# High and low weight parts interleaved in one buffer, at a walking place

## The chip, the cores and the metric

The program runs on one core of one Trainium2 chip. The metric is the device time in microseconds (us) of one execution; smaller is better.

## The reference

One row of 256 tokens of width 2048 passes through two blocks. The first mixes four branches (a gated linear attention, a gated linear recurrence, a compressed and sliding attention, a delta-rule recurrence), gates and sums them, and adds a convolved, gated feed-forward layer of width 5632. The second has two layers, each with two kinds of attention. All numbers are float32. Nearly all the arithmetic is products of the normalized activations with large weight matrices:

```
w_in     2048 x 16016      (all branches' inputs, and the four gates of 2048)
w_branch 4 x 512 x 2048    w_out 2048 x 2048
ffn_up   2048 x 11264      ffn_down 5632 x 2048
w_in_2   2 x 2048 x 2048   w_out_2 2 x 512 x 2048
y = rms_norm(x, g) @ w_in;  ...;  x = x + merged @ w_out;  x = x + ffn(x);  ...
```

## The kernel before

Activations lie transposed: features on the 128 partitions, tokens along the free dimension. To keep float32 accuracy at the rate of the shorter format `F32R`, each operand is split into a high part (the value rounded to `F32R`) and a low part (what is left), and a product is formed as high x high + high x low + low x high. For activations both parts lie in one tile: `act` is [128, 16, 2, 256], with part 0 high and part 1 low; `ys`, `ff_s` and `l_ys` are built alike.

Weights come from HBM in pieces of 128 partitions x 1024 floats (512 KB), packed beforehand in the order of use, by the generator `wchunk`. For each piece it issues a DMA on SP's queue into `raw` (four buffers), lets ScalarE write the high part `hi` (tile name `whi`, line 311 by way of `cp_s`), and lets VectorE write the low part `lo` = raw - hi (tile name `wlo`, line 299 by way of `tt`). `hi` and `lo` are separate tiles, three buffers each, 1088 floats per partition; a piece uses 1024 of them, from a starting place that `where` chooses. A buffer is written again once its last reader is done. The scheduler places these instructions by a priority that `rank` sets, so that the splitting runs ahead of the products.

`gemmT` uses the pieces as stationary operands, 128 weight columns at a time, with the activations as the moving operand. In the wide form (`w_gate`, `ffn_up`, `ffn_down`, `w_out`) one product moves both parts of the activations, 512 columns, past the high weights, and one moves the high part, 256 columns, past the low weights: a pair. In the narrow form (mixer inputs, branch outputs, second block) there are three products of 256 columns: a triple. Every product loads its weights anew. A piece of 1024 columns holds eight such pairs or triples. All products go through `mm`, line 293, into PSUM tiles `o`. `half_out` and the end of `proj_out` take pieces and form triples in the same way.

`gemm_tok` is the other way round: the activations are stationary and the pieces move, 512 columns at a time (272 in the case of one matrix), each activation block three times. It calls `wchunk` without a form.

`where` gives the starting places of `hi` and `lo` in floats. A table `AT` holds, for each activation tile, the place of that tile modulo 256 bytes; the places of the parts are at fixed distances from it, 64 and 192 bytes in the narrow form, 192 and 0 in the wide one. Without a form both are 0.

In between, as Python generators advanced by `tick` after each k, stand the small products and elementwise chains of the branches (`rwkv`, `lru`, `gla2`, `nsa2`, the attentions). One of them is of use below: in `gla2`, `factors` forms differences and products over halves of blocks of length L; at its last level, L = 1, its operands are every second float.

Of the kernel before, what the change touches and what calls it, by code (L numbers as in the profile page):

```python
# [9 lines left out]
F32R = mybir.dt.float32r  # L10
# [245 lines left out]
class Net:  # L256
# [100 lines left out]
    def wchunk(self, src, nk, n, form=None):  # L357

        kp = max(1, 1024 // n)
        if len(self.boot) > 4:  # L360
            kp = 2
        for k0 in range(0, nk, kp):
            kn = min(kp, nk - k0)
            for _ in range(kn // 2 if self.boot else 0):
                self.boot.pop(0)()
            with self.rank(20 * self.place):
                raw = self.raw.tile([128, 1024], F32, tag="raw", name="raw")[:, :kn * n]
                self.nc.sync.dma_start(raw, src[:, k0 * n:(k0 + kn) * n])
                a, b = self.where(form)
                hi = self.ws.tile([128, 1088], F32R, tag="hi", name="whi")[:, a:a + kn * n]  # L370
                lo = self.ws.tile([128, 1088], F32R, tag="lo", name="wlo")[:, b:b + kn * n]
                self.cp_s(hi, raw)
                self.tt(lo, raw, hi.bitcast(F32), OP.subtract)
            if self.place >= 0:
                self.place = self.place + 1 if self.place < 20 else -1
            yield k0, hi.rearrange("p (k n) -> p k n", n=n), lo.rearrange("p (k n) -> p k n", n=n)


    AT = {"act": 128, "ff_s": 224, "ys": 224, "l_ys": 160}

    def where(self, form):

        if form is None:
            return 0, 0
        name, wide = form
        return tuple((self.AT[name] + d) % 256 // 4 for d in ((192, 0) if wide else (64, 192)))

    def gemmT(self, src, act=None, wide=False, name="act"):

# [1355 lines left out]
```

## Time and profile before

| | |
|---|---|
| median of 2 runs | 1925.53 us (1925.04 to 1926.01) |
| the profiled execution's own time | 1919.65 us |
| its span, first to last instruction | 1917.8 us |
| busy: TensorE / its weight loads / VectorE / ScalarE / GpSimd | 98% / 89% / 73% / 54% / 4% |
| granted TensorE clock | 0.995 |
| read from HBM | 343.52 MB, 181 GB/s over the span |

The profiled execution is one run of the program under the hardware profiler. Busy shares are shares of the span. Matmuls overlap one another in the records, so the rate of TensorE is read from the distance between starts and not from durations.

### The profile page before, as it was taken

Reading aid. Unit: us, or ns where it says so; the run is one execution under the profiler, and the core shown is the slowest. Engines: PE = TensorE matmul, PEld = TensorE weight load, DVE = VectorE, ACT = ScalarE, POOL = GpSimd, SP = SyncE. Lnnn points to the kernel's source line nnn. Section 1 sums busy time; section 2 is a strip of 40 time slices with the busy share of each in tenths; the row PEclk is TensorE's granted clock in tenths of the full one; section 3 lists DMA queues with packets and bytes.
Section 4 is the critical chain, followed back from the end, with each engine's and each line's share of the span. In section 5 each row is a group of like instructions: output and inputs, shape, how many; then the busy total and the mean of one; then the engine's idle time right before and its main releaser. Section 6 shows DMA issues by size and latency. Waiting matters only on the chain.

```text
span 1917.8 us, 31880 instructions
## 1 busy us (share of the span) xinstructions
PE 1878.6 (98%) x12558; PEld 1701.4 (89%) x12558; DVE 1407.4 (73%) x2211; ACT 1034.8 (54%) x1542; POOL 80.9 (4%) x107
## 2 busy tenths in 40 slices
PE   8999999999999999999999999999999999999997
PEld 8999889999789999988888888888888888999886
DVE  8888967687776666675888787556888876768766
ACT  6565444465555444454655555334555554546574
POOL 0000010000000000002000000000000011003002
PEclk9999999999999999999999999999999999999999
DMA  7545553355644555565556555555555555654533
GB/s 273 188 154 181 193 143 111 121 167 169 225 144 150 191 196 190 196 230 192 194 193 193 197 191 193 195 193 188 197 195 194 192 196 193 210 165 152 192 124 108
DMA packets 98262, 348.48 MB, mean 182 GB/s; under 512 B 11200, under 2 KB 12224, under 8 KB 97984
## 3 DMA queue, kind: packets, MB, share of 16 engines
q1 hardware_dynamic: 93888, 336.15, 52.7%
q10 hardware_dynamic: 3600, 8.73, 1.3%
q0 software_dynamic: 624, 1.57, 0.4%
q8 instruction: 98, 1.61, 0.4%
q14 instruction: 52, 0.43, 0.1%
HBM read 343.52 MB, written 2.88 MB: 181 GB/s over the span
## 4 chain that ended last, share of the span: by engine, by line
PE 90%; DVE 5%; ACT 3%; DMA 1%; issue 1%; SPq 0%; POOL 0%; DVEq 0%; ACTq 0%
PE o L293 83%; DVE wlo L299 2%; ACT whi L311 1%; ACT L308 1%; DMA nsa_w<-in_cmp 1%; PE rw_u L293 0%; PE lg L1313 0%; PE rw_y L293 0%; PE rw_p L293 0%; PE gla_s L293 0%; DVE x L299 0%; PE l_o L293 0%; PE pt L318 0%; PE nsa_o L293 0%; PE rw_n L293 0%
## 5 line engine op out<-in xcount | busy, mean ns | idle before, releaser
L293 PE MATMUL o<-act,whi 128*128 128x512 f32 (+1 forms) x4736 | 1293.9, 344 | 6.0 <-ACT whi L311 6.0
L299 DVE TENSOR_TENSOR wlo<-raw,whi 128x1024 fp32r<-128x1024 f32 (+2 forms) x634 | 770.3, 1216 | 366.3 <-ACT whi L311 356.9
L293 PE MATMUL o<-act,wlo 128*128 128x256 f32 x3712 | 1034.3, 279 | 4.6 <-DVE wlo L299 4.5
L311 ACT CAST whi<-raw 128x1024 fp32r<-128x1024 f32 (+2 forms) x634 | 659.5, 1041 | 645.0 <-PE o L293 522.1
L293 PEld LDWEIGHTS o<-act,whi 128*128 128x128 f32 x4736 | 819.1, 189 | 113.8 <-ACT whi L311 6.5
L293 PEld LDWEIGHTS o<-act,wlo 128*128 128x128 f32 x3712 | 699.3, 188 | 9.5 <-DVE wlo L299 7.5
L293 PE MATMUL o<-ff_s,whi 128*128 128x512 f32 x704 | 239.5, 389 | 0.0
L293 PE MATMUL o<-ff_s,wlo 128*128 128x256 f32 x704 | 194.3, 276 | 0.0
L293 PEld LDWEIGHTS o<-ff_s,whi 128*128 128x128 f32 x704 | 132.2, 188 | 27.1
L293 PEld LDWEIGHTS o<-ff_s,wlo 128*128 128x128 f32 x704 | 132.2, 188 | 0.0
L299 POOL TENSOR_TENSOR acc<-acc,sq 128x256 f32<-128x256 f32 x56 | 58.7, 1049 | 1230.8 <-ACT sq L308 1228.6
L311 ACT COPY evh<-o 128x256 f32<-128x256 f32 x152 | 56.4, 371 | 97.9 <-PE o L293 97.8
L293 PE MATMUL o<-ys,whi 128*128 128x256 f32 x512 | 92.3, 280 | 0.0
L299 DVE TENSOR_TENSOR evh<-o,evh 128x256 f32<-128x256 f32 x152 | 64.0, 421 | 34.9 <-ACT evh L311 34.8
L293 PEld LDWEIGHTS o<-ys,whi 128*128 128x128 f32 x512 | 78.1, 188 | 1.9 <-issue 0.6
L293 PE MATMUL o<-whi,act 128*128 128x512 f32 (+1 forms) x256 | 74.0, 371 | 0.0
L305 DVE SCALAR_TENSOR_TENSOR ff_u<-hup,vec,ff_u 128x256 f32<-128x256 f32 x176 | 73.4, 479 | 0.0
L293 PE MATMUL o<-ys,wlo 128*128 128x256 f32 x256 | 71.7, 280 | 0.0
L308 ACT ACT_TABLE_LOAD x48 | 61.6, 1283 | 2.0 <-PEq L1733 1.2
L299 DVE TENSOR_TENSOR x<-o,x 128x256 f32<-128x256 f32 (+1 forms) x113 | 45.5, 454 | 14.5 <-PE o L293 8.9
L293 PEld LDWEIGHTS o<-whi,act 128*128 128x128 f32 x256 | 46.4, 188 | 8.8 <-issue 0.5
L308 ACT ACTIVATE ff_u<-hup,vec 128x256 f32<-128x256 f32 x88 | 48.0, 592 | 2.0 <-DVE hup L299 2.0
(427 smaller groups left out, 1407.9 us busy)
## 6 DMA issues: line engine op xcount, KB each, us to landing
raw<-in_ffn_up SPq DMA_DIRECT2D x176, 512.0 KB, 3.6
raw<-in_w_gate SPq DMA_DIRECT2D x128, 512.0 KB, 3.9
raw<-in_w_mix SPq DMA_DIRECT2D x78, 512.0 KB, 3.7
raw<-in_ffn_down SPq DMA_DIRECT2D x48, 512.0 KB, 3.4
raw<-in_w SPq DMA_DIRECT2D x48, 512.0 KB, 3.7
raw<-in_w_br SPq DMA_DIRECT2D x32, 512.0 KB, 4.3
raw<-in_w_out SPq DMA_DIRECT2D x32, 512.0 KB, 4.4
raw<-in_ffn_down2a SPq DMA_DIRECT2D x32, 512.0 KB, 3.5
```

The costliest lines, as they stand in the source:

```text
L293: self.nc.tensor.matmul(out, lhsT, rhs, start=start, stop=stop, skip_group_check=True)
L299: (eng or self.nc.vector).tensor_tensor(out, a, b, op=op)
L305: self.nc.vector.scalar_tensor_tensor(out, a, s, b, op0=op0, op1=op1)
L308: self.nc.scalar.activation(out, a, f, **k)
L311: self.nc.scalar.copy(out, a)
```

## The change

`hi` and `lo` become two views of one tile of [128, 1056, 2]: float 2i of a partition is the high part of weight i, float 2i + 1 its low part. Both are so read and written by steps of 8 bytes. The tile has three buffers, as each of the two had. `where` now returns one place, in pairs of 8 bytes: the activation tile's own place plus 40 bytes for each piece that has asked before, modulo 256 bytes; so 32 consecutive pieces of `gemmT`, `half_out` and `proj_out` start at 32 different places. Pieces without a form stay at 0.

```diff
-                a, b = self.where(form)
-                hi = self.ws.tile([128, 1088], F32R, tag="hi", name="whi")[:, a:a + kn * n]
-                lo = self.ws.tile([128, 1088], F32R, tag="lo", name="wlo")[:, b:b + kn * n]
+                a = self.where(form)
+                both = self.ws.tile([128, 1056, 2], F32R, tag="hl", name="whl")[:, a:a + kn * n]
+                hi, lo = both[:, :, 0], both[:, :, 1]
                 self.cp_s(hi, raw)
                 self.tt(lo, raw, hi.bitcast(F32), OP.subtract)
...
+    count = 0
     AT = {"act": 128, "ff_s": 224, "ys": 224, "l_ys": 160}
 
     def where(self, form):
 
         if form is None:
-            return 0, 0
-        name, wide = form
-        return tuple((self.AT[name] + d) % 256 // 4 for d in ((192, 0) if wide else (64, 192)))
+            return 0
+        self.count += 1
+        return (self.AT[form[0]] + 8 * (5 * self.count % 32)) % 256 // 8
```

## Rows read from the trace of the kernel before

**Rows 1.** The page's first part: busy us (share of the span) xinstructions.
```profile
PE 1878.6 (98%) x12558; PEld 1701.4 (89%) x12558; DVE 1407.4 (73%) x2211; ACT 1034.8 (54%) x1542; POOL 80.9 (4%) x107
```
**Rows 2.** The page's fourth part, the chain that ended last, by line.
```profile
PE o L293 83%; DVE wlo L299 2%; ACT whi L311 1%; ACT L308 1%; DMA nsa_w<-in_cmp 1%; PE rw_u L293 0%; PE lg L1313 0%; PE rw_y L293 0%; PE rw_p L293 0%; PE gla_s L293 0%; DVE x L299 0%; PE l_o L293 0%; PE pt L318 0%; PE nsa_o L293 0%; PE rw_n L293 0%
```
**Rows 3.** TensorE's groups by line and form: xcount | busy us, mean ns | idle before.
```profile
L293 PE MATMUL o<-act,wlo 128*128 128x256 f32 x3712 | 1034.3, 279 | 4.6 <-DVE wlo L299 4.5
L293 PE MATMUL o<-act,whi 128*128 128x512 f32 x2688 | 928.3, 392 | 0.0
...
L293 PE MATMUL o<-ff_s,whi 128*128 128x512 f32 x704 | 239.5, 389 | 0.0
L293 PE MATMUL o<-ff_s,wlo 128*128 128x256 f32 x704 | 194.3, 276 | 0.0
...
L293 PE MATMUL o<-ys,wlo 128*128 128x256 f32 x256 | 71.7, 280 | 0.0
L293 PE MATMUL o<-whi,act 128*128 128x512 f32 x192 | 60.6, 394 | 0.0
...
L293 PE MATMUL o<-wlo,act 128*128 128x512 f32 x96 | 37.9, 394 | 0.0
L293 PE MATMUL o<-l_ys,wlo 128*128 128x256 f32 x128 | 35.5, 277 | 0.0
```
**Rows 4.** Timeline of TensorE, wide form, starts 24 pairs apart: start us, us, what.
```profile
899.82 0.39 PE L293 MATMUL o<-act,whi 128*128 128x512 f32 x1
...
907.98 0.39 PE L293 MATMUL o<-act,whi 128*128 128x512 f32 x1
```
**Rows 5.** The core's span and mean granted TensorE clock.
```profile
core 0: 1917.8 us, clock 0.995
```
**Rows 6.** Timeline of TensorE: three triples, four, then `act` pairs: three, four.
```profile
545.65 0.40 PE L293 MATMUL o<-ys,whi 128*128 128x256 f32 x2
...
546.72 0.39 PE L293 MATMUL o<-ys,whi 128*128 128x256 f32 x2
...
548.08 0.39 PE L293 MATMUL o<-ys,whi 128*128 128x256 f32 x2
...
548.42 0.40 PE L293 MATMUL o<-act,whi 128*128 128x512 f32 x1
...
549.48 0.39 PE L293 MATMUL o<-act,whi 128*128 128x512 f32 x1
...
550.84 0.39 PE L293 MATMUL o<-act,whi 128*128 128x512 f32 x1
```
**Rows 7.** Timeline of TensorE, wide form, starts eight pairs apart.
```profile
556.55 0.40 PE L293 MATMUL o<-act,whi 128*128 128x512 f32 x1
...
559.35 0.40 PE L293 MATMUL o<-act,whi 128*128 128x512 f32 x1
```
**Rows 8.** The tile `whi`, 900 to 1600 us: ns min/median/max; idle us, times, until.
```profile
L299 DVE TENSOR_TENSOR wlo<-raw,whi x258: 1209/1226/1229, 899.7 to 1599.7; 128x1024 fp32r<-128x1024 f32 x129
L311 ACT CAST whi<-raw x257: 1032/1050/1056, 901.3 to 1598.6; 128x1024 fp32r<-128x1024 f32 x129
its engine sat idle before it (us, times) until:
  PE o L293: 195.0, 131
```
**Rows 9.** The tile `gla_E`, all levels L together: ns min/median/max.
```profile
L299 DVE TENSOR_TENSOR gla_E<-gla_b x16: 412/418/425, 414.0 to 439.7; 128x256 f32<-128x256 f32 x16
```
**Rows 10.** Who waited for whom on TensorE: us in total, times, longest us.
```profile
PE o L293 <- ACT whi L311: 6.0, 2, 5.3
PE o L293 <- DVE wlo L299: 4.7, 7, 0.9
```
**Rows 11.** Timeline of TensorE in `gemm_tok`, starts 12 products apart.
```profile
1812.83 0.62 PE L293 MATMUL o<-whi,act 128*128 128x512 f32 x2
...
1815.61 0.39 PE L293 MATMUL o<-whi,act 128*128 128x512 f32 x1
```

## The prediction

> **What bounds the kernel now.** I began with the page's busy times: TensorE is busy 98% of the span, VectorE 73%, ScalarE 54% [rows 1]. Since a busy TensorE need not be one at its peak, I went on to the chain that ended last: 83% of the span is TensorE in line 293 on the output tiles `o`, which are the weight products [rows 2]. The groups by line and form give their number and sort [rows 3]: 2688 + 704 = 3392 wide pairs (a high product of 512 columns and a low one of 256) and, from the remaining low products, 3712 + 704 + 256 + 128 - 3392 = 1408 narrow triples (high, high, low, 256 columns each). Both come to 768 columns, so I speak of 4800 groups. Besides them 288 products of `gemm_tok` have the weights as the moving operand, 512 columns each; 96 more, by the code (16 k, two token halves, three products), have 272.
>
> The time of a group is read in the timeline from start to start, since durations overlap. In the long even stretch 24 wide pairs take 907.98 - 899.82 = 8.16 us, 340 ns each [rows 4]. [...] Yet a triple at its best also takes 340 ns: four in 548.08 - 546.72 = 1.36 us [rows 6]. So 340 ns is what the moving stream of 768 four-byte columns costs when nothing disturbs it. 4800 x 0.340 = 1632 us: most of the kernel already stands at this floor.
>
> But the same instructions also run slower, and this is what matters here. Behind a pause eight wide pairs take 559.35 - 556.55 = 2.80 us, 350 ns each [rows 7]. In one `ys` gemm the first three triples take 546.72 - 545.65 = 1.07 us (357 ns each), the next four 340; the wide pairs behind it take 353 for three, then 340 [rows 6]. Instructions, sizes and places are the same; only the moment at which weight load and moving stream meet differs. The products find their even step after a few groups, or they don't. I read it as a dependence on how the two reads of SBUF stand to each other; the code's fixed places modulo 256 bytes hold that relation constant from piece to piece.
>
> **The change, part by part.** No instruction, byte of HBM or DMA is added or removed. What changes is the step of four accesses from 4 to 8 bytes (ScalarE's write of the high part, VectorE's read of it and its write of the low part, TensorE's read of both), the place of a piece relative to the moving operand (40 bytes further each piece, all 32 places in 32 pieces), and that the two parts come free together.
>
> *Splitting.* The cast takes 1.05 us and the subtraction 1.23 us per piece [rows 8], while a piece feeds TensorE for 8 x 0.34 = 2.72 us. VectorE's steps of 8 bytes are shown: the GLA factor products include one level (L = 1) that reads and writes every second float, and all 16 calls lie between 412 and 425 ns [rows 9]. So 0 for VectorE. ScalarE has no such row; between nothing and a doubled cast (2.1 us, still inside 2.72; 1035 + 634 x 1.05 = 1700 us in all, under the span) I take nothing, as VectorE's row is the nearest. The cover is the lead of three buffers: over the whole run TensorE waits 6.0 us for high parts and 4.7 us for low ones [rows 10], and of 257 casts in the middle of the run 131 had to wait until TensorE freed a buffer [rows 8], so they run as far ahead as the buffers let them. Taking both parts as one buffer means that a high product may wait until the low part is written, about 1.2 us later; with such a lead that is hidden nearly everywhere. If it isn't in the lean pieces, I put it at up to 12 us, twice the wait for high parts. Taken: 0.
>
> *Weight load by steps of 8 bytes.* A load of 128 weights now covers 1024 bytes of a partition instead of 512. No load in this trace is strided. The nearest row is the moving stream: it sustains 256 x 4 = 1024 bytes in 113 ns (340/3). If the load's port does the same, the load still fits behind a 256-column product, just; if it fetches half as fast (227 ns), it is exposed behind every 256-column product. That would be 113 ns in a pair and 3 x 113 = 340 in a triple: 383 + 479 = 862 us. These are the ends; I am near the low one, because the moving stream's row is the same memory and engine at the same rate. [...]
>
> *The walking place.* What held the even step was a fixed relation; now each piece (8 groups) brings another. Bounds: all pieces fall in step at once, 0; none does, 4800 x 10 ns (350 against 340) = 48 us, or 58 us at 352; three groups lost per piece and then the even step, about 40 ns x 602 pieces = 24 us. The load also meets the moving stream on twice as many bytes, so up to twice that, some 115 us. Weight load and walking place are two readings of one contention, not to be added in full: I take **52 us** for both.
>
> [...]
>
> *Weights as the moving operand.* In `gemm_tok` 12 products take 1815.61 - 1812.83 = 2.78 us, 232 ns each [rows 11]; these pieces were unplaced before and still are. Read by steps of 8 bytes they sweep 4096 bytes, twice the rate that any row shows. Ends: nothing, and doubled, 288 x 0.232 = 67 us plus 96 x 272/512 x 0.232 = 12 us, 79 us in all. No row is near; I take the low end for the sum and keep the other as a rival.
>
> **Sum.** 0 + 0 + 52 + 0 = 52 us. On the profiled execution's own time of 1919.65 us (span 1917.8 and 1.85 around it): 1971.7. The median shown, 1925.53, is 5.9 above that execution: 1977.6, say **1978 us**, 2.7% slower. About 2% (38 us) is what a measurement here tells from no change.
>
> **The rivals.**
> (1) Not slower. The loads keep pace and each piece falls in step within a group or two: 0 to 30 us, 1923 to 1955. For it: steps of 8 bytes cost VectorE nothing, the even step was reached from several starts [rows 6]. Against it: eight pairs in a row without finding the step [rows 7]. [...] It decides at 8 ns a group (38 us over 4800): below that, no difference.
> (2) Dearer, 2010 to 2080. The moving read at 8 bytes halves in `gemm_tok` (+79, so 2005 alone and 2057 with my 52), or the contention doubles with the bytes (+115, 2041). For it: no row shows TensorE reading SBUF faster than 9 bytes per ns. Against: `gemm_tok` is 79 us in all, and doubling it is the worst case.
> (3) The load halves: 1925.5 + 862 = 2788 us. For it: no strided load is in the trace. Against: the stream's rate.
> [...]
> (5) That the change doesn't do what it says: buffers of 1056 x 8 = 8448 bytes are 33 x 256, so the places do walk through all 32; only a starting tile off the 256-byte grid would shift them all alike, which walking makes indifferent.
>
> **How the numbers follow.** Forecast (1960 to 2010) 0.40; dearer (2) 0.20; not slower (1) 0.27; load halved (3) 0.08; faster (4) 0.05. The range leaves out (3), (4) and a little at the edges: 1920 to 2075. Faster by over 2%: 0.05. Within 2%: 0.27. Slower: 0.40 + 0.20 + 0.08 = 0.68.
>
> **What would show it.** TensorE's counts unchanged. In the timeline of the feed-forward part wide pairs at 345 to 355 ns in place of 340, changing from piece to piece; triples at 115 to 120 ns a product. If pairs stay at 340 everywhere, the walking term is wrong; if low products stretch to 227, rival (3) holds; if `gemm_tok` goes well past 232 ns, rival (2). Casts over 1.2 us or subtractions over 1.4 us would refute the first term, and TensorE waits on `whi` or `wlo` far above 11 us the cover. I would be most wrong if a strided weight load has a price that no row here hints at.

## The result, and the profile after

The changed kernel takes 2048.4 us (2046.92 to 2049.89) against 1925.53: a ratio of 1.0638 (95% interval 1.0592 to 1.0684), 6.4% slower. Its span is 2048.1 us against 1917.8 [rows 5], 130 us more, at the same granted clock of 0.995.

The page's busy times of the changed kernel come first, then its chain of waits by line:

```profile
PE 2014.5 (98%) x12558; PEld 1785.9 (87%) x12558; DVE 1415.7 (69%) x2211; ACT 1092.0 (53%) x1542; POOL 81.9 (4%) x107
...
PE o L293 85%; DVE whl L299 1%; ACT whl L311 1%; DMA x<-in_xT 1%; DMA nsa_w<-in_cmp 1%; ACT L308 0%; PE rw_u L293 0%; PE lg L1314 0%; PE rw_y L293 0%; PE rw_p L293 0%; PE gla_s L293 0%; PE l_o L293 0%; PE nsa_o L293 0%; DVE x L299 0%; PE rw_n L293 0%
```

The counts are those of [rows 1], and the bound is the same: TensorE in the weight products [rows 2]. So the same instructions run slower, and three rows of the chain say which. A row of the chain is an unbroken run of one group: its start, its length and the number of products. Before:

```profile
91.61 16.36 PE o L293 x144
...
937.14 391.77 PE o L293 x2304
...
1656.62 34.02 PE o L293 x198
```

After, the same 144, 2304 and 198 products:

```profile
95.31 17.34 PE o L293 x144
...
992.68 406.32 PE o L293 x2304
...
1739.11 55.91 PE o L293 x198
```

The first row is narrow: 16.36/144 = 113.6 ns a product became 120.4, so a triple went from 341 to 361. The second is wide: 391.77/1152 = 340.1 ns a pair became 352.7. The third holds the 96 products of one `gemm_tok`, and it alone lost 22 us. The groups by line and form of the changed kernel (compare [rows 3]) name them:

```profile
L293 PE MATMUL o<-act,whl 128*128 128x256 f32 x5760 | 1152.2, 285 | 9.3 <-ACT whl L311 5.5 <-DVE whl L299 3.7
L293 PE MATMUL o<-act,whl 128*128 128x512 f32 x2688 | 958.2, 399 | 0.0
...
L293 PE MATMUL o<-whl,act 128*128 128x512 f32 x288 | 131.0, 634 | 0.0
...
L293 PE MATMUL o<-whl,act 128*128 128x272 f32 x96 | 24.6, 446 | 0.0
```

A product with moving weights now lasts 634 ns instead of 394, and in the timeline 39 of them stand in one even row; without the last one's own 0.63 us that is (17.86 - 0.63)/38 = 453 ns from start to start, against 232 [rows 11]:

```profile
197.46 17.86 PE L293 MATMUL o<-whl,act 128*128 128x512 f32 x39
```

The splitting is as good as unchanged: the tile `whl` between 900 and 1600 us (compare [rows 8]), and what TensorE waited for (compare [rows 10]):

```profile
L311 ACT CAST whl<-raw x248: 1106/1133/1173, 899.8 to 1599.8; 128x1024 fp32r<-128x1024 f32 x124
L299 DVE TENSOR_TENSOR whl<-raw,whl x247: 1211/1228/1232, 906.3 to 1598.2; 128x1024 fp32r<-128x1024 f32 x124
its engine sat idle before it (us, times) until:
  PE o L293: 196.4, 131
```

```profile
PE o L293 <- ACT whl L311: 5.5, 1, 5.5
...
PE o L293 <- DVE whl L299: 3.7, 4, 1.9
```

Where the 130 us went follows from adding up, over the whole trace, the distance from each product's start to the next one's, by kind (us; the waits behind a product are in its distance). The columns are before, after, and four of the experiments below:

```
                          before   after   tok_apart  walk_only   still   one_buffer
pairs                     1168.9  1203.8     1203.3     1196.6   1202.7      1172.2
triples                    525.3   549.1      548.1      535.6    544.1       526.8
gemm_tok                    80.8   154.5       80.8       81.0    154.5        80.8
everything else            128.0   125.4      126.5      125.7    125.6       125.8
```

After minus before: pairs +34.9, triples +23.8, `gemm_tok` +73.7, the rest -2.6.

### The profile page after: what moved, and what is told of

It reads as the page before. It is cut to its first block, busy times and chain, and to the rows that moved or that the text cites. A ratio compares the mean times of both kernels' runs of the same rounds, so it can differ in the third digit from the quotient of the medians.

```text
span 2048.1 us, 31873 instructions
## 1 busy us (share of the span) xinstructions
PE 2014.5 (98%) x12558; PEld 1785.9 (87%) x12558; DVE 1415.7 (69%) x2211; ACT 1092.0 (53%) x1542; POOL 81.9 (4%) x107
## 4 chain that ended last, share of the span: by engine, by line
PE 91%; DVE 3%; ACT 3%; DMA 2%; issue 1%; POOL 0%; SPq 0%; DVEq 0%; ACTq 0%; POOLq 0%
PE o L293 85%; DVE whl L299 1%; ACT whl L311 1%; DMA x<-in_xT 1%; DMA nsa_w<-in_cmp 1%; ACT L308 0%; PE rw_u L293 0%; PE lg L1314 0%; PE rw_y L293 0%; PE rw_p L293 0%; PE gla_s L293 0%; PE l_o L293 0%; PE nsa_o L293 0%; DVE x L299 0%; PE rw_n L293 0%
## 5 line engine op out<-in xcount | busy, mean ns | idle before, releaser
L293 PE MATMUL o<-act,whl 128*128 128x256 f32 (+1 forms) x8448 | 1370.9, 321 | 9.3 <-ACT whl L311 5.5
L293 PEld LDWEIGHTS o<-act,whl 128*128 128x128 f32 x8448 | 1229.1, 197 | 116.1 <-issue 7.2
L311 ACT CAST whl<-raw 128x1024 fp32r<-128x1024 f32 (+2 forms) x634 | 713.8, 1126 | 747.4 <-PE o L293 604.3
L299 DVE TENSOR_TENSOR whl<-raw,whl 128x1024 fp32r<-128x1024 f32 (+2 forms) x634 | 772.4, 1219 | 483.8 <-ACT whl L311 479.0
L293 PE MATMUL o<-ff_s,whl 128*128 128x512 f32 (+1 forms) x1408 | 248.6, 339 | 0.0
L293 PEld LDWEIGHTS o<-ff_s,whl 128*128 128x128 f32 x1408 | 222.1, 196 | 26.2
L293 PE MATMUL o<-whl,act 128*128 128x512 f32 (+1 forms) x384 | 155.6, 587 | 0.0
L293 PEld LDWEIGHTS o<-whl,act 128*128 128x128 f32 x384 | 79.2, 207 | 73.4 <-issue 70.2
L293 PE MATMUL o<-ys,whl 128*128 128x256 f32 x768 | 102.4, 287 | 0.0
L293 PEld LDWEIGHTS o<-ys,whl 128*128 128x128 f32 x768 | 96.7, 198 | 2.0 <-issue 1.0
```

Of the source, the lines that this page charges most:

```text
L293: self.nc.tensor.matmul(out, lhsT, rhs, start=start, stop=stop, skip_group_check=True)
L299: (eng or self.nc.vector).tensor_tensor(out, a, b, op=op)
L311: self.nc.scalar.copy(out, a)
```

## The experiments

Theory A: TensorE itself pays for reading by steps of 8 bytes, the moving weights of `gemm_tok` with half their rate, the stationary weights with some ns per load. Its rivals are named with each run.

**1. `gemm_tok` contiguous again** (`e1_tok_apart`), all else as changed:

```diff
...
+                if form is None:
+                    flat = whl.rearrange("p n t -> p (n t)")
+                    hi, lo = flat[:, 0:kn * n], flat[:, 1024:1024 + kn * n]
...
```

> The changed kernel, but the pieces of gemm_tok (weights as the moving operand) keep high and low parts as two runs of floats side by side in the same buffer; all other pieces stay interleaved and walk. Theory A (a read by steps of 8 bytes costs TensorE as such, and the moving operand of gemm_tok is hit by half its rate): gemm_tok products return from 453 to about 232 ns, 73.7 us less in all, 1970 to 1980 us. Rival (the products of gemm_tok are slow because of the buffer shared by both parts or of a wait, not of the step): they stay at 453 ns and the time near 2048 us.

Measured: 1975.4 us, ratio to the kernel before 1.0276 (1.0256 to 1.0295). The chain's third row is back, the second is not:

```profile
961.41 406.32 PE o L293 x2304
...
1707.84 34.69 PE o L293 x198
```

So the 74 us belong to the layout of moving weights: same buffer, same release, only the step taken away.

**2. The walk alone** (`e2_walk_only`), on the kernel before, contiguous parts:

```diff
...
+        self.count += 1
+        step = 8 * (5 * self.count % 32)
-        return tuple((self.AT[name] + d) % 256 // 4 for d in ((192, 0) if wide else (64, 192)))
+        return tuple((self.AT[name] + d + step) % 256 // 4 for d in ((192, 0) if wide else (64, 192)))
```

> The kernel before with its two tiles, contiguous parts, and only the place walking: 40 bytes further for each piece, high and low parts alike. Theory A (the step of 8 bytes sets the price of the placed products): groups fall back into 340 ns at most places, some places cost, 1925 to 1955 us in all. Rival B (what costs is that the place walks): groups at 350 to 360 ns as in the changed kernel, about 1980 us. gemm_tok at 232 ns under both.

Measured: 1956.6 us, ratio 1.0184 (1.0163 to 1.0206). The narrow and the wide row of its chain:

```profile
93.79 16.98 PE o L293 x144
...
952.07 402.66 PE o L293 x2304
```

Pairs at 349.5 and triples at 354 ns: neither theory as it stood. Walking alone costs pairs and triples 38 us of the 59. I sorted the groups of this trace by the place of their piece (third and later groups of each piece): pairs average 340.8 ns at the old place and 347 to 354 at the 31 others; triples 340.4 and 340.8 at two places, 128 bytes apart, and 348 to 360 elsewhere. So one place in 32, or two, hold the even step. Theory A had it found again from most places; it isn't.

**3. Interleaved, standing still** (`e3_still`):

```diff
-        self.count += 1
-        return (self.AT[form[0]] + 8 * (5 * self.count % 32)) % 256 // 8
+        return self.AT[form[0]] % 256 // 8
```

> The changed kernel with the walking taken out: every piece starts at the place of its activation tile. Theory A (the step sets the price): pairs stay at 349 to 357 ns and triples at 353 to 366, gemm_tok at 453, 2030 to 2065 us. Rival B (the walking sets the price): pairs and triples at 340, the 59 us gone, about 1990 us.

Measured: 2043.1 us, ratio 1.0629 (1.0611 to 1.0648). The same rows of its chain:

```profile
95.03 17.28 PE o L293 x144
...
987.39 407.05 PE o L293 x2304
```

Pairs at 353.3, triples at 360: rival B falls, as standing still doesn't bring 340 back. With interleaved parts it hardly matters whether the place walks (52.6 us in pairs and triples, against 58.7). Sorted in the same way, the trace of the changed kernel has no place at 340: pairs average 349 to 357, triples 353 to 370.

**4. One buffer, parts contiguous** (`e4_one_buffer`), old places:

```diff
...
+                both = self.ws.tile([128, 2, 1088], F32R, tag="hl", name="whl")
+                hi, lo = both[:, 0, a:a + kn * n], both[:, 1, b:b + kn * n]
```

> The kernel before with both parts in one tile of 2 x 1088 floats, each part contiguous and at its old place: only the common release and the common tile are left of the change. Theory A: no price, 1920 to 1935 us, TensorE's waits on whl under 15 us. Rival C (a product of the high part now waits for the low part's subtraction, or buffers come free later): waits on whl of 20 us and more, 1950 us.

Measured: 1922.2 us, ratio 0.9999 (0.9989 to 1.0009). The chain's long row and the waits:

```profile
940.23 391.77 PE o L293 x2304
```

```profile
PE o L293 <- ACT whl L311: 5.9, 2, 5.3
PE o L293 <- DVE whl L299: 5.4, 7, 1.9
```

The common tile and release cost nothing; rival C is out.

**5. Steps of 16 bytes** (`e5_step16`):

```diff
-        self.ws = self.P("ws", ctx, 3)
+        self.ws = self.P("ws", ctx, 2)
...
-                both = self.ws.tile([128, 1056, 2], F32R, tag="hl", name="whl")[:, a:a + kn * n]
+                both = self.ws.tile([128, 1024, 4], F32R, tag="hl", name="whl")[:, a:a + kn * n]
...
-        return (self.AT[form[0]] + 8 * (5 * self.count % 32)) % 256 // 8
+        return (self.AT[form[0]] + 8 * (5 * self.count % 32)) % 256 * 0
```

> The changed kernel with a float in four in use (steps of 16 bytes in place of 8), every piece at place 0, and two buffers for the pieces instead of three (more waits between pieces are expected from that; the products inside a piece are what is read). Theory A (TensorE goes through a row of SBUF at about 9 bytes of its length per ns, used or not: 512 x 4 bytes in 227 ns, 512 x 8 in 453): 512 columns in gemm_tok take 906 ns; a load of 128 weights goes over 2048 bytes and takes 227 ns, so pairs 454 and triples 680 ns, some 3000 us or more in all. Rival (the price is for a step wider than 4 bytes, whatever its width): gemm_tok 453, pairs 353, triples 360, about 2050 us. A third case, the load's port slower than the stream's: pairs above 500 ns.

Measured: 3038.8 us, one run. Its chain (144 narrow products), its weight loads, its splitting, and a stretch of `gemm_tok`:

```profile
169.85 33.95 PE o L293 x144
```

```profile
L293 PEld LDWEIGHTS o<-act,whl 128*128 128x128 f32 x8448 | 2018.4, 325 | 85.7 <-DVE whl L299 65.8 <-issue 7.1 <-ACT whl L311 7.0
```

```profile
L311 ACT CAST whl<-raw x163: 2022/2061/2090, 899.8 to 1597.2; 128x1024 fp32r<-128x1024 f32 x163
L299 DVE TENSOR_TENSOR whl<-raw,whl x163: 2018/2044/2074, 901.9 to 1599.3; 128x1024 fp32r<-128x1024 f32 x163
```

```profile
344.56 8.02 PE L293 MATMUL o<-whl,act 128*128 128x512 f32 x17
```

A narrow product takes 33.95/144 = 236 ns (227 expected), a pair 469 (the medians 350 and 119 of its two distances; 454 expected): two loads one after the other. A load now takes about 235 ns, where one at 8 bytes kept up with products 120 ns apart, and it sets the pace. In the weight loads' own group it lasts 325 ns, where the kernel before has 189 and the changed one 197:

```profile
L293 PEld LDWEIGHTS o<-act,whi 128*128 128x128 f32 x4736 | 819.1, 189 | 113.8 <-ACT whi L311 6.5 <-issue 4.1 <-DVE act L305 0.2
...
L293 PEld LDWEIGHTS o<-act,whl 128*128 128x128 f32 x8448 | 1229.1, 197 | 116.1 <-issue 7.2 <-ACT whl L311 5.8 <-DVE whl L299 5.1
```

But the moving weights did not follow: without the last one's own 0.65 us, (8.02 - 0.65)/16 = 461 ns, next to 453 at 8 bytes and far from 906. So "9 bytes of a row's length per ns" is wrong for the moving operand. For the loads its figures came close. That the total came near 3000 us says little: the term for `gemm_tok` failed, and TensorE's waits for pieces came to 28.2 us, against 9.2 in the changed kernel.

**6 and 7. High and low parts at places of their own**, 64 combinations 32 bytes apart, interleaved with `gemm_tok` contiguous (`e6_places_apart`) and in the tiles of before (`e7_places_contiguous`). The interleaved one:

```diff
...
+        c = self.count
+        return tuple((self.AT[form[0]] + 32 * d) % 256 // 8 for d in (c % 8, c // 8 % 8))
...
+                    hi, lo = whl[:, a:a + kn * n, 0], whl[:, b:b + kn * n, 1]
```

> Interleaved as in the changed kernel, with gemm_tok's pieces contiguous, and the places of high and low parts now independent: all 64 combinations of 8 by 8 places, 32 bytes apart, piece by piece. Theory A (the step of 8 bytes costs at every place): no combination below 347 ns a pair and 352 a triple; 1965 to 1985 us. Rival D (the price is that high and low parts share one place, where the kernel before had 128 or 64 bytes between them): some combinations at 340 ns.

> The same 64 combinations of places with the contiguous tiles of the kernel before. After the run with the walk alone (340 ns at one place of 32 in pairs, at two in triples): a few of the 64 combinations at 340 ns, among them the ones of the kernel before (192 and 0 bytes for pairs, 64 and 192 for triples), the rest 345 to 360; 1945 to 1960 us. Were the even step a matter of the distance between high and low parts alone, eight combinations along a diagonal would have it.

Measured: 1975.6 and 1958.2 us, one run each. The long wide row of the first, then of the second:

```profile
961.32 406.14 PE o L293 x2304
```

```profile
952.55 402.83 PE o L293 x2304
```

Groups sorted by the two places (mean ns from start to start, third and later groups of a piece; places in bytes from that of the activation tile):

```
                                            pairs            triples
interleaved, all 64 combinations            347 to 360       356 to 364
contiguous, high at 192, low at 0           341.0            353.4
contiguous, high at 64, low at 64           352.2            340.4
contiguous, high at 64, low at 192          352.1            343.2
contiguous, high at 0, low at 0             351.1            359.9
contiguous, the other 60                    344 to 354       347 to 365
```

Rival D falls: none of these 64 combinations rescues the interleaved layout. In the contiguous one, one combination of 64 serves pairs, the kernel's own (`where`: 192 and 0), and two serve triples: the kernel's own, 64 and 192, and 64 and 64. The two places don't settle it alone, however: triples at 192 and 64, which run 2 had near 341 (its second place, 128 bytes on), stand at 356 here, and why isn't shown. A contiguous load at a poor place is as dear as a strided one: 351 and 360 at 0 and 0, against 353 and 360 with interleaved parts at that place (run 3). Run 8 will show the same on a whole kernel.

**8. Alternating blocks** (`e8_blocks`); a small class hands out column slices of the cut tile:

```diff
...
+                a, m = self.where(form)
+                flat = self.ws.tile([128, 2112], F32R, tag="hl", name="whl")[:, a:a + 2 * kn * n]
+                cut = flat.rearrange("p (q t m) -> p q t m", t=2, m=m)
+                hi, lo = cut[:, :, 0], cut[:, :, 1]
...
+            return 0, (4, 8, 2, 16)[(self.tok - 1) // 8]
...
+        return self.AT[form[0]] // 4, 128
```

> One tile, high and low parts alternating in blocks: the four uses of gemm_tok have blocks of 4, 8 (the one of 272 columns), 2 and 16 floats, in this order; all other pieces have blocks of 128 floats, so that each load is contiguous, at the place of the activation tile. Theory A as length per ns (4096 bytes of a row are gone through, used or not): all uses of gemm_tok at 453 ns for 512 columns and 241 for 272. Rival E (what counts is the number of 16-byte stretches that are touched): blocks of 4, 8 and 16 floats at 232 and 125 ns as before, only blocks of 2 floats at 453.

Measured: 1984.4 us, one run. The class moves line 293 to 304. The timeline of `gemm_tok` with blocks of 4, 8 (272 columns), 2 and 16 floats:

```profile
198.82 8.48 PE L304 MATMUL o<-whl,act 128*128 128x512 f32 x36
...
473.62 3.55 PE L304 MATMUL o<-whl,act 128*128 128x272 f32 x24
...
1718.54 11.97 PE L304 MATMUL o<-whl,act 128*128 128x512 f32 x26
...
1868.76 6.43 PE L304 MATMUL o<-whl,act 128*128 128x512 f32 x26
```

By the distances from start to start (with pauses left out): 232, 125, 453 and about 240 ns. Blocks of sixteen are slightly slower than blocks of four; why isn't shown. Blocks of four floats go through the same 4096 bytes of a row as steps of 8 bytes and lose nothing; blocks of two lose half. So the length of row is not the measure: rival E holds, as far as it goes. By its own count of 16-byte stretches, however, run 5 (512 of them) should have taken twice as long as this kernel's blocks of two (256), and it took 461 ns. What the runs bear out is narrower: four adjacent floats at a time go at the full rate (232 ns), the three looser layouts (pairs, single floats by 8 and by 16 bytes) at about half of it (453, 453 and 461 ns), and steps of 16 bytes are only 2% slower than steps of 8.

This run also holds a control for run 3: its loads are contiguous, with high and low parts at the activation tile's place, as run 3 has them interleaved. The narrow and the wide row of its chain:

```profile
94.47 17.27 PE o L304 x144
...
952.58 404.27 PE o L304 x2304
```

That is 360 ns a triple and 350.9 a pair, against 360 and 353.3 in run 3. Added up as in the table above, pairs take 1193.7 and triples 545.5 us, 45 more than before, where run 3 has 53: the poor place alone accounts for 45, the step for some 8 more.

**9 to 11. A load with room to hide**, high products alone in the wide form: interleaved and walking (`e9_high_only`, on run 1), the kernel before (`e10_high_only_before`), and that with the walk (`e11_high_only_walk`):

```diff
-                                    start=(k == 0), stop=False)
+                                    start=(k == 0), stop=(k == total - 1))
...
-                        self.mm(d, lo[:, kk, c], a[:, 0], start=False, stop=(k == total - 1))
+                        if not wide:
+                            self.mm(d, lo[:, kk, c], a[:, 0], start=False, stop=(k == total - 1))
...
-                self.tt(lo, raw, hi.bitcast(F32), OP.subtract)
+                if form is None or not form[1]:
+                    self.tt(lo, raw, hi.bitcast(F32), OP.subtract)
```

> Interleaved and walking, gemm_tok's pieces contiguous, and in the wide form the low products and the subtraction that feeds them left out (the output lacks high activations x low weights there). What is read is the distance of 512-column products inside a piece, each with one load of 128 weights that has 227 ns of room. Theory F (a strided load takes time from the moving stream, about 6 ns each, hidden or not): 233 to 236 ns. Rival G (a strided load takes 120 ns and costs only where a 256-column product is too short to hide it): 227 ns. The whole time says little, since pieces are then used up faster than they are made; 1600 to 1750 us.

> The kernel before with the same products and subtractions left out: control for the run before it. 227 ns a product inside a piece under both theories, unless the even step needs the low products too: then 228 to 233.

> The kernel before with the place walking by 40 bytes and contiguous parts, the same products and subtractions left out. Theory F (loads and stream disturb each other where their places don't fit, contiguous loads less than strided ones): 228 to 234 ns. Rival G: 227 ns, as a contiguous load is hidden as well.

Measured: 1589.2, 1558.5 and 1576.2 us, one run each. Runs 10 and 11 leave out the same products as run 9. The same 1166 products in the chains of 9, 10 and 11:

```profile
821.88 270.76 PE o L293 x1166
```

```profile
803.17 267.06 PE o L293 x1166
```

```profile
811.90 270.87 PE o L293 x1166
```

232.2, 229.0 and 232.3 ns. Rival G expected 227 in the first and the last, where the load has 227 ns of room: it fails, a load that could hide still costs the stream some 5 ns. The pairs of the changed kernel say the same: inside a piece the 512-column product went from 227 to 235 ns from start to start, the 256-column one from 113 to 118 (medians). Theory F's second half fails too: the contiguous load off its place takes as much as the strided one. The control doesn't hold the even step either (a tenth of its distances is at 226, the median at 229), so this place, tuned for pairs, isn't the right one without the low products; the strided load's own share can't be read finer than the 3 ns between the rows.

## Why the prediction was right and wrong

*The bound and the splitting* were right. TensorE paces both kernels; VectorE's subtraction is unchanged at 1.23 us, ScalarE's cast went from 1.05 to 1.13, under the limit of 1.2 that was set, and TensorE's waits for pieces sum to 9.2 us against 10.7. That a common tile costs nothing was shown by run 4 alone.

*Weight load and walking place*, 52 us: measured 34.9 + 23.8 = 58.7. The size held, but in part by luck: no run shows 52 us as a price of the strided load, only some 8 us beside the 45 of a poor place (runs 3 and 8). Of the 12 to 13 ns that a pair lost, 8 lie on its 512-column product, where the load has 227 ns of room. Of the two readings, neither is the whole. The walk alone costs 38 us (run 2), interleaving without the walk 53 (run 3), contiguous parts at the place of run 3 cost 45 (run 8), walk and interleaving together 59. This fits a single loss: each takes away the place at which loads and stream don't disturb each other, and it can be lost only once. My bound "all pieces fall in step at once" was wrong about its cause: I took the recovery after three groups [rows 6] for something that happens from many starts, while it happened at the kernel's own places, and not always there [rows 7]. And a strided load of 120 ns (rival G) would fit the measured triple (3 x 120.4), but this is no evidence for it: contiguous loads at a poor place give 120 as well (runs 7 and 8), and loads with room to hide disturb too (runs 9 to 11). What distinguishes the strided load is that none of the places tried frees it.

*Weights as the moving operand*, the step that failed: "I take the low end for the sum and keep the other as a rival". Between 0 and 79 us with no row near, 0 was taken; the trace shows 73.7, and run 1 that undoing the layout there gives it back. The prediction had noted that these reads would need twice the 9 bytes per ns that any row shows, and that was reason not to take nothing: at 9 bytes per ns 4096 bytes are 455 ns, and 453 were measured. With 52 + 79 the forecast would have been about 2057. Yet runs 5 and 8 show that this rate isn't the law behind the number: blocks of four floats go through the same 4096 bytes in 232 ns.

*The step itself* costs each access differently. VectorE's subtraction takes 1.23 us at 4 and at 8 bytes and 2.04 at 16 (run 5); ScalarE's cast 1.05, 1.13 and 2.06; the load stands behind products 120 ns apart at 8 bytes and 236 at 16. The moving operand falls to about half its rate at 8 bytes already, 453 ns against 232, and takes 461 at 16. And loading weights is not free for the running product: pairs go from 341 to as much as 354 ns with the places of run 7, and loads with room to hide cost some 5 ns each in runs 9 and 11. What it is that load and stream share is not shown.

*Rivals:* (2) came true in its first form, 2057 against 2048, and term by term: 79 us against 73.7, 52 against 58.7. (3), the load halved, happened, but at 16 bytes. (1), (4), the faster one, and (5) did not.

## What to carry to other kernels

Where one layout change reaches an operand in two roles, price the roles apart: here 384 moving products cost more than 11,000 stationary ones (73.7 us against 58.7). Where a change asks a read for a rate that no row shows, don't put the term at nothing; which end is right is for a run to say, since the blocks of four floats in run 8 went through the same 4096 bytes in 232 ns. And when a kernel runs at a floor that depends on places, as this one does (pairs at 341 ns at one place of 32 in run 2, at 347 to 354 elsewhere), expect a change of place or step to lose it; undoing one of two such changes can give little back (6 us of 59 without the walk, 21 without the step), so they have to be tested apart.

## What the runs showed of the hardware

- A moving fp32r operand: 512 columns in 227 to 232 ns when contiguous or in blocks of four adjacent floats, about 240 in blocks of sixteen, 453 in single floats by 8 bytes or in blocks of two, 461 by 16 bytes (the kernel before, the changed one, runs 5 and 8). Blocks that start off a 16-byte boundary were not tried.
- A load of 128 fp32r weights: the record lasts 189 ns contiguous, 197 by 8 bytes, 325 by 16 (the kernel before, the changed one, run 5); only the last sets the pace (236 ns a product).
- Load and moving stream disturb each other by place: of 64 combinations of places of high and low weights, 32 bytes apart, one gave pairs 341 ns, and two gave triples 340 and 343; the rest went up to 354 and 365 (run 7). Why those places is not settled by these runs, nor is the place the whole of it (192 and 64: 341 in run 2, 356 in run 7).
- ScalarE's cast and VectorE's subtraction of 1024 elements: 1.13 and 1.23 us by 8 bytes (the changed kernel), 2.06 and 2.04 by 16 (run 5).
